# Expert sums, gates and selection by quarters instead of halves in a hybrid decoder with a product-key expert layer

## Chip, cores and metric

One core of one Trainium2 chip runs the whole program. The metric is device time in microseconds of one execution; the kernel before was timed three times, and its median is the number that the change is compared with. All profile rows come from one further execution, recorded by the hardware profiler.

## What is computed

Two layers; each adds a token mixer and an expert network to the residual stream `h` of 1040 tokens (16 meta tokens and 1024 real ones) by 1024 features. The mixer is left alone by the change. The expert network is this, cut from the reference:

```python
q = (xt @ wq).reshape(t, PEER_HEADS, 2, PEER_HALF)              # 8 heads, 2 halves of a key
s = jnp.einsum('thpd,hpnd->thpn', q, sub_keys)                  # 64 scores per half
s_top, i_top = lax.top_k(s, PEER_TOPK)                          # best 16 of each half
cand_s = s_top[:, :, 0, :, None] + s_top[:, :, 1, None, :]      # 256 sums
best_s, best_j = lax.top_k(cand_s..., PEER_TOPK)                # best 16 pairs = experts
g = jax.nn.softmax(best_s, axis=-1)
h_all = jnp.einsum('td,nd->tn', xt, u)                          # all 4096 experts
a = jax.nn.gelu(take_along_axis(h_all, idx)) * g
w = zeros((t, N_EXPERTS)).at[..., idx].add(a)
return w @ v
```

The kernel computes `gelu(xt @ u.T)` for all 4096 experts, multiplies it by a gate matrix that holds `g` at the chosen experts and 0 elsewhere, and multiplies the product by `v`.

## The kernel before

Tokens lie along the free dimension, in four quarters: 272 (with the meta tokens), 256, 256, 256 tokens; in the last layer the meta tokens are dropped and all four have 256. Two quarters form a half of the sequence, called `P` (the first two) and `Q` (the last two). All large products are made of three matmuls each, with operands split into a high and a low part of 32 bits (`wh`, `wl` for weights, `ah`, `al` for the gated hidden values). A weight block of 128x512 is loaded by `wpiece` (L296): the first time, ACT copies the high part (L273), POOL or DVE subtracts (L280, the engine is chosen by `split_on`) and the low part is also stored to DRAM (L292); at later times the block is loaded again, ACT copies the high part (L307) and the low part is loaded from DRAM (L310). All these transfers are issued from SP, in order.

For each half, in this order:

- `scores` (L960) computes the key scores of two heads for all token tiles.
- `route` (L987) works on DVE for two heads and all token tiles of the half: per tile and key half a top-16 search of five instructions (L997 to L1001), candidate sums (L1013 to L1020), a top-16 search over 64 candidates, softmax (the exponential is on ACT, L1032), and index arithmetic on 128x2048 arrays (L1067, L1070, L1074). It writes the expert's number in two parts, `mS` and `rS`, and the gate `gS`. There are four calls per half.
- `hidden` (L1094) makes `gelu(xt @ u.T)` in 32 row tiles of 128 experts, in one 512-wide matmul per step where both quarters have 256 tokens, else in a 272-wide and a 256-wide one. The result goes to the array `G` (L1113).
- `slots` (L1117) transposes `mS`, `rS`, `gS` by PE.
- `gates` (L1133) makes the gate matrix for 16 tokens: DVE compares with a ramp (L1142, 128x2048; L1144, 128x512) and multiplies by the high and the low part of the gates (L1146, L1147); PE multiplies the two one-hot matrices for each token. For `P` these are 32 matmuls of 32 columns (L1171); ACT copies the result, in part into a side tile, and POOL multiplies that into `G` (L1177). For `Q` (`wide`) they are 16 matmuls of 64 columns (L1159), and ACT and DVE (L1165) add two parts. Rows of `G` that `hidden` makes after the gate get multiplied by POOL (L1111). Calls of `gates` are spread over the rows of `hidden` from row 17 (`P`) or row 6 (`Q`) on.
- `values_steps` (L1185) sums over the experts: for four of the eight output tiles at a time it goes through the 32 rows of `G`, splits a row of both quarters (L1203 on ACT, L1204 on DVE), loads one `v` block of 128x512 and accumulates in PSUM (L1209). After the 32 rows the residual is updated (`hupdate`, L258).

The sum of `P` carries the normalisation (`apply`), the `scores` and the `route` calls of `Q` beside it, as pieces of a generator; `tc.issue_after` ties a piece to the subtraction of an earlier row (`LAG`), and `BUD` says how much of it may follow each row. The order of instructions within an engine's queue is otherwise chosen by a planner that follows a simulated timeline and takes ready work by its place in the program. Each queue then runs in that order. In the first layer the sum of `Q` is cut in two, with part of the next layer's projection between; in the last layer its second part is done for one quarter after the other, with the final normalisation behind.

```python
for r in range(32):                                               # values_steps
    wh, wl = wpiece(v_w[l][:, r, d0 * 128:d0 * 128 + 512], f"v{l}_{r}_{d0}" if reuse else None)
...
while cst and P.gated < P.sp.w and P.gated * (end - lo) < P.sp.w * (r + 1 - lo):   # hidden
    gates(P, G, *cst)
```

## Time and profile before

| | |
|---|---|
| median of 3 runs | 3380.03 us (3378.39 to 3394.43) |
| profiled execution | 3392.98 us, its span 3391.3 us |
| PE busy | 3157.8 us (93%) |
| DVE, ACT, POOL busy | 2172.3, 1381.1, 1091.0 us |
| mean granted clock of TensorE | 0.955 |
| moved by DMA | 651.27 MB, mean 192 GB/s |

The busy times are unions of recorded spans. A matmul's recorded span is longer than its distance to the next one, because matmuls overlap in the engine; the pace is read from rows that give the length of an unbroken series and its count. The span less the PE's busy time is 234 us; a granted clock below 1 in a stretch is a second kind of loss, which the busy time hides. The stretches of the expert network are, in us from the start: `hidden` of `P` 798 to 1061 and 2452 to 2724, sum of `P` 1061 to 1320 and 2724 to 2969, `hidden` of `Q` 1320 to 1535 and 2969 to 3182, sum of `Q` 1535 to 1800 (with a projection) and 3182 to the end.

### The profile page before, as it was taken

Reading aid. Unit: us, or ns where it says so; the run is one execution under the profiler, and the core shown is the slowest. Engines: PE = TensorE matmul, PEld = TensorE weight load, DVE = VectorE, ACT = ScalarE, POOL = GpSimd, SP = SyncE. Lnnn points to the kernel's source line nnn. Section 1 sums busy time; section 2 is a strip of 40 time slices with the busy share of each in tenths; the row PEclk is TensorE's granted clock in tenths of the full one; section 3 lists DMA queues with packets and bytes.
Section 4 is the critical chain, followed back from the end, with each engine's and each line's share of the span. In section 5 each row is a group of like instructions: output and inputs, shape, how many; then the busy total and the mean of one; then the engine's idle time right before and its main releaser. Section 6 shows DMA issues by size and latency. Waiting matters only on the chain.

```text
span 3391.3 us, 64331 instructions
## 1 busy us (share of the span) xinstructions
PE 3157.8 (93%) x22459; PEld 2647.5 (78%) x22459; DVE 2172.3 (64%) x7020; ACT 1381.1 (41%) x3278; POOL 1091.0 (32%) x1092
## 2 busy tenths in 40 slices
PE   7999999989788989999898999999898889999998
PEld 6686887679788988787775868876776678688788
DVE  4645446579896589663326454455698957976547
ACT  4534334433334434444344343344333344344355
POOL 4314022224475232131401231223245643313325
PEclk9899999989889999999997999999898899999999
DMA  8767774564324555445964687755753256554555
GB/s 284 236 202 247 257 245 146 174 217 164 125 88 158 182 178 189 163 152 191 331 232 151 210 274 241 232 170 167 251 173 125 94 179 221 183 189 151 180 173 156
DMA packets 397222, 651.27 MB, mean 192 GB/s; under 512 B 43536, under 2 KB 109152, under 8 KB 396896
## 3 DMA queue, kind: packets, MB, share of 16 engines
q1 hardware_dynamic: 396896, 647.16, 59.3%
q8 instruction: 176, 2.88, 0.4%
q14 instruction: 150, 1.23, 0.1%
HBM read 489.56 MB, written 157.42 MB: 191 GB/s over the span
## 4 chain that ended last, share of the span: by engine, by line
PE 59%; DVE 23%; DMA 6%; ACT 2%; issue 2%; POOL 1%; SPq 0%; POOLq 0%; DVEq 0%; ACTq 0%
PE b L1209 14%; PE b L1104 13%; PE b L334 12%; PE b L980 4%; DVE arena L1142 2%; DMA arena<-h 2%; PE b L704 2%; DVE arena_r L1204 2%; PE b L1159 2%; DVE arena L998 2%; DVE arena L999 2%; PE b L758 1%; DVE arena L1001 1%; PE b L619 1%; DVE arena L1147 1%
## 5 line engine op out<-in xcount | busy, mean ns | idle before, releaser
L280 POOL TENSOR_TENSOR arena_r<-arena,arena_r 128x512 fp32r<-128x512 f32 (+1 forms) x453 | 561.0, 1246 | 867.9 <-ACT arena_r L273 813.9
L1104 PE MATMUL b<-arena_r 128*128 128x512 f32 (+2 forms) x3840 | 782.3, 363 | 23.4 <-ACT arena L1113 13.5
L1209 PE MATMUL b<-arena_r 128*128 128x512 f32 (+2 forms) x4224 | 755.4, 337 | 36.5 <-DVE arena_r L1204 24.7
L1209 PEld LDWEIGHTS b<-arena_r 128*128 128x128 f32 x4224 | 643.8, 190 | 135.8 <-DVE arena_r L1204 41.9
L1104 PEld LDWEIGHTS b<-arena_r 128*128 128x128 f32 x3840 | 643.5, 197 | 123.4 <-ACT arena L1113 14.1
L334 PE MATMUL b<-arena_r 128*128 128x256 f32 (+1 forms) x4992 | 694.6, 293 | 33.8 <-ACT arena_r L273 10.2
L334 PEld LDWEIGHTS b<-arena_r 128*128 128x128 f32 x4992 | 635.1, 193 | 74.4 <-issue 21.8
L273 ACT ACTIVATE arena_r<-arena 128x512 fp32r<-128x512 f32 x456 | 285.1, 629 | 472.4 <-PE b L1104 124.4
L1204 DVE TENSOR_TENSOR arena_r<-arena,arena_r 128x512 fp32r<-128x512 f32 (+2 forms) x352 | 260.5, 751 | 230.9 <-ACT arena_r L1203 230.1
L307 ACT ACTIVATE arena_r<-arena 128x512 fp32r<-128x512 f32 x284 | 178.5, 631 | 327.4 <-PE b L1209 130.5
L980 PE MATMUL b<-arena_r 128*128 128x256 f32 (+1 forms) x1632 | 220.6, 291 | 15.3 <-DMA arena_r<-m_0l 5.3
L1142 DVE TENSOR_TENSOR arena<-arena 128x2048 f16<-128x2048 f16 x129 | 178.8, 1388 | 83.8 <-PE b L1159 83.7
L980 PEld LDWEIGHTS b<-arena_r 128*128 128x128 f32 (+1 forms) x1632 | 205.4, 190 | 27.9 <-DMA arena_r<-m_0l 7.3
L1177 POOL TENSOR_TENSOR arena<-arena 128x448 f32<-128x448 f32 (+20 forms) x129 | 144.2, 1123 | 150.8 <-DVE arena L1165 115.4
L1203 ACT ACTIVATE arena_r<-arena 128x512 fp32r<-128x512 f32 (+2 forms) x352 | 171.7, 502 | 25.2 <-PE b L1209 23.6
L256 POOL TENSOR_TENSOR arena<-arena 128x256 f32<-128x256 f32 (+2 forms) x105 | 90.7, 864 | 271.4 <-ACT arena L255 264.2
L280 DVE TENSOR_TENSOR arena_r<-arena,arena_r 128x256 fp32r<-128x256 f32 (+1 forms) x187 | 101.0, 546 | 92.1 <-ACT arena_r L273 71.2
L716 DVE TENSOR_TENSOR_SCAN arena<-arena,zf 128x384 f32<-128x384 f32 (+6 forms) x116 | 104.3, 903 | 79.0 <-ACT arena L711 77.8
L1111 POOL TENSOR_TENSOR arena<-arena 128x272 f32<-128x272 f32 (+25 forms) x86 | 95.1, 1110 | 158.4 <-DVE arena L1165 141.0
L422 ACT ACTIVATE arena<-b 128x256 f32<-128x256 f32 (+1 forms) x144 | 55.3, 384 | 202.0 <-PE b L334 201.2
L577 POOL TENSOR_TENSOR arena<-arena,mhalf 128x8 f32<-128x8 f32 (+3 forms) x43 | 63.6, 1479 | 210.5 <-DVE arena L574 143.3
L1171 PE MATMUL b<-arena 128*128 128x32 f16 x2080 | 83.5, 192 | 34.2 <-DVE arena L1142 15.9
(273 smaller groups left out, 4240.8 us busy)
## 6 DMA issues: line engine op xcount, KB each, us to landing
arena<-in_v_w_dram SPq DMA_DIRECT2D x288, 256.0 KB, 2.9
arena<-in_u_pk_dram SPq DMA_DIRECT2D x256, 256.0 KB, 3.0
arena_r<-a_0h SPq DMA_DIRECT2D x108, 256.0 KB, 3.7
arena_r<-a_0l SPq DMA_DIRECT2D x108, 256.0 KB, 4.0
arena_r<-a_1h SPq DMA_DIRECT2D x108, 256.0 KB, 3.3
arena_r<-a_1l SPq DMA_DIRECT2D x108, 256.0 KB, 3.9
arena<-m SPq DMA_DIRECT2D x92, 256.0 KB, 4.3
arena<-in_w_pk_dram SPq DMA_DIRECT2D x72, 256.0 KB, 4.3
```

The costliest lines, as they stand in the source:

```text
L273: ACT.activation(hi, src, AF.Copy)
L280: e.tensor_tensor(lo[:, a:b], src[:, a:b], hi[:, a:b].bitcast(F32), op=ALU.subtract)
L307: ACT.activation(hi, wload(src), AF.Copy)
L334: PE.matmul(ps, wt[:, ks], x.at(low, k, xo, sp.w), start=(k == 0 and i == 0), stop=(k == KT - 1 and i == 2))
L716: DVE.tensor_tensor_scan(keep[0:m, 0:wd][:, ::-1], keep[0:m, 0:wd][:, ::-1], zf[0:m, 0:1].to_broadcast([m, wd]), keep[0:m, wd:wd + 1], op0 ...
L980: PE.matmul(ps, yv(half, low, k, oo, m), wt[:, kk * 256:kk * 256 + 256], start=(k == 0 and i == 0 and e == 0), stop=(k == KT - 1 and i == ...
L1104: PE.matmul(ps, wt[:, ks], yv(h, low, k, 0, w // 2 if h is None else w), start=(k == 0 and i == 0), stop=(k == KT - 1 and i == 2))
L1142: DVE.tensor_tensor(Lh, iotaM.unsqueeze(1).to_broadcast([128, 4, 128, 4]), v4(P.mT, 128), op=ALU.is_equal)
L1177: POOL.tensor_tensor(G[:, 0:n, t0:t0 + 16], gt[:, 0:n], G[:, 0:n, t0:t0 + 16], op=ALU.mult)
L1203: ACT.activation(ah, G[:, r, o:o + w], AF.Copy)
L1204: last = DVE.tensor_tensor(al, G[:, r, o:o + w], ah.bitcast(F32), op=ALU.subtract)
L1209: PE.matmul(ps, wt[:, d * 128:d * 128 + 128], pr[low], start=(opens and r == 0 and i == 0), stop=(closes and r == 31 and i == 2))
```

## The change

Selection and gates are now made for one quarter at a time, and the sums too. In detail:

- `route` becomes `tops(P, half, cc)` (the first searches) and `combine(P, half, cc)` (the rest), each for four heads and the tiles of one quarter ("half" in the code is the first or second quarter of `P` or `Q`). The candidates and index arrays keep about their size: four heads by two or three tiles in place of two heads by four or five.
- Before `hidden` of `P` stands the selection of the first quarter alone. After 15 rows of `hidden` come `slots` of the first quarter and then `tops`, `combine`, `tops` of the second one; the gates of the first quarter are spread over rows 15 to 31.
- `values(l, P, G, half, ...)` sums one quarter. A 256-token quarter accumulates all eight output tiles in one pass over `G` (two tiles share a PSUM bank), so a row of `G` is split once and two `v` blocks are loaded per row; a 272-token quarter and the last quarter of all take two passes of four tiles.
- The sum of the first quarter carries `second`: the last `combine`, `slots` and all 16 calls of `gates` of the second quarter, plus `apply` for the third quarter. The sum of the second quarter carries `apply` for the fourth, the `scores` of `Q` and the selection of `Q`'s first quarter. `Q` goes the same way. In the last layer the final normalisation of three quarters runs beside the last sum.
- `gates`: one multiplication of 128x1024 for both parts of the gates; always 32 matmuls of 32 columns; rows of `G` that exist already are multiplied straight from PSUM by DVE; the rest is copied by ACT. The POOL product and the `wide` form go.
- PSUM rings, tile sizes and `BUD` (0.3 to 2.3), `PR` (17 to 15), `PEND` (29 to 31) change with it; `scores` copies two tiles of scores with one ACT instruction.

The core of the diff:

```diff
-    set_rings(d=(0, 1), o=(2,), a=(3, 4, 5, 6, 7), h=(0, 1, 6, 7), g=(2, 3), s=(2, 3, 4, 5), v=(4, 5, 6, 7, 2, 3))
+    set_rings(d=(0, 1), o=(2,), a=(3, 4, 5, 6, 7), h=(6, 7, 2, 3), g=(0, 1), s=(4, 5), v=(4, 5, 6, 7, 2, 3))
...
+    def gates(P, half, G, iotaM, iotaR):
...
+        R = sb([128, 4, 2, 32, 4], F16, "R")
+        DVE.tensor_tensor(R, R0.unsqueeze(2).to_broadcast([128, 4, 2, 32, 4]),
+                          P.gg[half][:, t0 // 4:t0 // 4 + 4].unsqueeze(3).to_broadcast([128, 4, 2, 32, 4]), op=ALU.mult)
...
         if n:
-            POOL.tensor_tensor(G[:, 0:n, t0:t0 + 16], gt[:, 0:n], G[:, 0:n, t0:t0 + 16], op=ALU.mult)
+            gv = G[:, 0:n, go:go + 16]
+            DVE.scalar_tensor_tensor(gv, pv[:, 0:n], 1.0 / GSC, gv, op0=ALU.mult, op1=ALU.mult)
...
+    def second(P, G, cst, tabs):
+        yield from combine(P, 1, 1, *tabs)
+        slots(P, 1)
+        yield 1.5
+        while P.gated[1] < P.parts[1][1].w:
+            gates(P, 1, G, *cst)
+            yield 3.0
+    def values(l, P, G, half, todo=iter(()), work=(), hs=None, group=8):
+        o, sp = P.parts[half]
+        w = sp.w
...
+        group = min(group, 4 if w > 256 else 8)
...
+        for d0 in range(0, 8, group):
...
+            for r in range(32):
...
+                done.append(DVE.tensor_tensor(al, G[:, r, o:o + w], ah.bitcast(F32), op=ALU.subtract).ins)
+                for d in range(group):
+                    if d % 4 == 0:
+                        wh, wl = wpiece(v_w[l][:, r, (d0 + d) * 128:(d0 + d) * 128 + 512], f"v{l}_{r}_{d0 + d}")
...
+                if len(done) > LAG:
+                    left = BUD * group / 8
+                    with tc.issue_after(done[-1 - LAG]):
+                        while left > 0:
+                            left -= next(todo, 99)
...
+            run(tops(P, 0, 0), combine(P, 0, 0, *tabs), tops(P, 0, 1))
+            scores(l, P, 3, (1,), "s")
+            run(combine(P, 0, 1, *tabs))
+        hidden(l, P, G, 0, PR, "h")
+        slots(P, 0)
+        run(tops(P, 1, 0), combine(P, 1, 0, *tabs), tops(P, 1, 1))
         hidden(l, P, G, PR, 32, "h", cst, PEND)
+        values(l, P, G, 0, second(P, G, cst, tabs), {20: lambda: apply(2 * l + 1, qs[2], gf, Y[0], rb)})
         Q = peer_setup(qs[2], qs[3])
...
+        values(l, P, G, 1, later(), work)
+        hidden(l, Q, G, 0, PR, "h")
+        slots(Q, 0)
+        run(tops(Q, 1, 0), combine(Q, 1, 0, *tabs), tops(Q, 1, 1))
+        hidden(l, Q, G, PR, 32, "h", cst, PEND)
...
+        values(l, Q, G, 0, second(Q, G, cst, tabs))
...
+        values(l, Q, G, 1, iter(()), {4 + 8 * i: lambda i=i: final(qs[i]) for i in range(3)}, hs, 4)
```

## Rows read from the trace of the kernel before

**Rows 1.** The page: span, and each engine's busy time, share and instructions

```profile
span 3391.3 us, 64331 instructions
...
PE 3157.8 (93%) x22459; PEld 2647.5 (78%) x22459; DVE 2172.3 (64%) x7020; ACT 1381.1 (41%) x3278; POOL 1091.0 (32%) x1092
```

**Rows 2.** Stretches: length, then PE, PEld, DVE, ACT, POOL busy, clock, DMA share, GB/s

```profile
798.00:1061.00 263.00, 224.61 (x2410) 219.85 (x2409) 232.00 (x648) 83.22 (x205) 151.32 (x109) 0.90 0.34 113
1061.00:1320.00 259.00, 243.62 (x1931) 237.78 (x1930) 195.31 (x931) 105.97 (x249) 89.11 (x68) 0.99 0.59 183
1320.00:1535.00 215.00, 212.65 (x1296) 172.90 (x1294) 146.65 (x439) 98.05 (x268) 62.32 (x72) 1.00 0.52 168
1535.00:1800.00 265.00, 253.36 (x1268) 210.02 (x1269) 84.78 (x140) 108.32 (x203) 44.29 (x60) 0.98 0.74 251
2452.00:2724.00 272.00, 232.62 (x1809) 187.31 (x1807) 245.01 (x748) 92.28 (x192) 153.41 (x112) 0.89 0.40 133
2724.00:2969.00 245.00, 235.08 (x1167) 192.50 (x1168) 188.99 (x882) 98.00 (x184) 90.20 (x64) 0.99 0.64 201
2969.00:3182.00 213.00, 210.82 (x1288) 172.35 (x1286) 146.02 (x418) 95.42 (x260) 60.94 (x60) 1.00 0.52 165
3182.00:3391.00 209.00, 194.50 (x1235) 174.54 (x1235) 124.51 (x214) 100.74 (x208) 65.76 (x70) 0.96 0.58 174
```

**Rows 3.** Timeline of PE: start, length and count of two unbroken series

```profile
1705.76 47.22 PE L1209 MATMUL b<-arena_r 128*128 128x512 f32 x204 [1.00 <-ACT arena_r L307]
...
3287.16 42.08 PE L1209 MATMUL b<-arena_r 128*128 128x256 f32 x356
```

**Rows 4.** Group on PE, 2592 to 2724 us: busy, mean ns, idle before, releasers

```profile
L1171 PE MATMUL b<-arena 128*128 128x32 f16 x1024 | 39.7, 192 | 17.5 <-DVE arena L1142 8.6 <-DVE arena L1147 6.2 <-DVE arena L1146 2.5
```

**Rows 5.** Shorter stretches, columns as in rows 2

```profile
1631.00:1706.00 75.00, 64.26 (x459) 59.00 (x458) 22.55 (x43) 29.11 (x59) 33.53 (x34) 0.98 1.00 357
2381.00:2452.00 71.00, 60.07 (x420) 56.90 (x420) 48.85 (x352) 24.25 (x50) 13.81 (x16) 0.89 0.81 261
2452.00:2570.00 118.00, 99.97 (x418) 78.80 (x416) 117.24 (x606) 43.09 (x68) 50.80 (x37) 0.93 0.51 170
2592.00:2724.00 132.00, 111.12 (x1301) 91.60 (x1299) 117.49 (x118) 44.19 (x114) 94.79 (x69) 0.86 0.31 102
```

**Rows 6.** Waits of ACT, 2452 to 2724 us: total us, times, longest

```profile
ACT arena L1032 <- DVE arena L1031: 33.2, 4, 13.9
```

**Rows 7.** Groups on DVE, 2592 to 2724 us, columns as in rows 4

```profile
L1142 DVE TENSOR_TENSOR arena<-arena 128x2048 f16<-128x2048 f16 x30 | 46.9, 1563 | 0.0
L1147 DVE TENSOR_TENSOR arena<-arena 128x512 f16<-128x512 f16 x30 | 28.9, 965 | 0.0
L1146 DVE TENSOR_TENSOR arena<-arena 128x512 f16<-128x512 f16 x30 | 27.4, 914 | 12.6 <-PE b L1171 12.5
L1144 DVE TENSOR_TENSOR arena<-arena 128x512 f16<-128x512 f16 x28 | 21.8, 804 | 0.1
```

**Rows 8.** Groups on DVE, 1370 to 1535 us, columns as in rows 4

```profile
L1142 DVE TENSOR_TENSOR arena<-arena 128x2048 f16<-128x2048 f16 x30 | 37.0, 1235 | 37.9 <-PE b L1159 37.8
L1146 DVE TENSOR_TENSOR arena<-arena 128x512 f16<-128x512 f16 x30 | 16.8, 558 | 0.0
...
L1165 DVE SCALAR_TENSOR_TENSOR arena<-b,arena 128x200 f32<-128x200 f32 x6 | 2.0, 354 | 0.5 <-ACT arena L1164 0.5
```

**Rows 9.** Groups on DVE, 1061 to 1320 us, columns as in rows 4

```profile
L1204 DVE TENSOR_TENSOR arena_r<-arena,arena_r 128x272 fp32r<-128x272 f32 x62 | 40.9, 661 | 29.3 <-ACT arena_r L1203 29.1
L1204 DVE TENSOR_TENSOR arena_r<-arena,arena_r 128x256 fp32r<-128x256 f32 x62 | 36.6, 590 | 3.4 <-ACT arena_r L1203 3.4
```

**Rows 10.** Group on POOL, 2724 to 2969 us, columns as in rows 4

```profile
L280 POOL TENSOR_TENSOR arena_r<-arena,arena_r 128x512 fp32r<-128x512 f32 x59 | 83.6, 1421 | 132.3 <-ACT arena_r L273 109.2 <-DMA arena<-in_v_w_dram 18.1 <-DMA arena_r<-m_3l 3.2
```

**Rows 11.** DMA issues over the whole span: count, KB each, median us to landing

```profile
arena<-in_v_w_dram SPq DMA_DIRECT2D x288, 256.0 KB, 2.9
```

**Rows 12.** Group on ACT over the whole span, columns as in rows 4

```profile
L307 ACT ACTIVATE arena_r<-arena 128x512 fp32r<-128x512 f32 x284 | 178.5, 631 | 327.4 <-PE b L1209 130.5 <-PE b L1104 90.7 <-issue 62.0
```

More of the change, by code (lines that the diff above doesn't have):

```diff
@@ L959, in scores @@
     def scores(l, P, c, halves, ring):
[L961 to L968 removed]
+        pairs = []
+        for half in halves:
+            tiles = list(enumerate(P.parts[half][1].tiles))
+            if len(tiles) == 3:
+                POOL.memset(sv(P, half, c)[:, 0], 0.0)
+                pairs.append((half, tiles[0:1]))
+            pairs.append((half, tiles[-2:]))
         bks = [ps1(ring) for _ in pairs]
@@ new lines, in scores, with top16 @@
+        for bk, (half, tiles) in zip(bks, pairs):
+            j, m, n = tiles[0][0], tiles[0][1][1], len(tiles)
+            ACT.activation(sv(P, half, c)[0:m, j:j + n], bk[0:m, 0:n * 256].rearrange("p (j a n) -> p j a n", a=4, n=64),
+                           AF.Copy)
+    def top16(s, val, idx):
+        DVE.max(val[:, 0:8], s)
+        DVE.max_index(idx[:, 0:8], val[:, 0:8], s)
+        DVE.match_replace(s, val[:, 0:8], s, -3.0e38)
+        DVE.max(val[:, 8:16], s)
+        DVE.max_index(idx[:, 8:16], val[:, 8:16], s)
@@ new lines, in tops, with combine @@
+    def tops(P, half, cc):
+        nt = len(P.parts[half][1].tiles)
+        V = sb([128, 3, 8, 16], F32, "V")
+        I = sb([128, 3, 8, 16], U32, "I")
+        P.V[half, cc] = V, I
+        for a in range(8):
+            for j in range(nt):
+                top16(sv(P, half, 2 * cc + a // 4)[:, j, a % 4, :], V[:, j, a], I[:, j, a])
+                yield 1.3
+    def combine(P, half, cc, startT, pidxT):
+        nt = len(P.parts[half][1].tiles)
+        ng = 4 * nt
+        V, I = P.V.pop((half, cc))
@@ L1114, in hidden, with slots @@
             P.rows = r + 1
-            while cst and P.gated < P.sp.w and P.gated * (end - lo) < P.sp.w * (r + 1 - lo):
-                gates(P, G, *cst)
-    def slots(P):
-        sp = P.sp
-        for j, (o, m) in enumerate(sp.tiles):
+            w0 = P.parts[0][1].w
+            while cst and P.gated[0] < w0 and P.gated[0] * (end - lo) < w0 * (r + 1 - lo):
+                gates(P, 0, G, *cst)
+    def slots(P, half):
+        for j, (o, m) in enumerate(P.parts[half][1].tiles):
             tp = ps1("g").bitcast(F16)[:, 0:256].rearrange("p (a b) -> p a b", a=2)
@@ new lines, in gates @@
+        R0 = sb([128, 4, 32, 4], F16, "R0")
+        DVE.tensor_tensor(R0, iotaR.unsqueeze(1).to_broadcast([128, 4, 32, 4]), v4(P.rT[half], 32), op=ALU.is_equal)
+        R = sb([128, 4, 2, 32, 4], F16, "R")
+        DVE.tensor_tensor(R, R0.unsqueeze(2).to_broadcast([128, 4, 2, 32, 4]),
+                          P.gg[half][:, t0 // 4:t0 // 4 + 4].unsqueeze(3).to_broadcast([128, 4, 2, 32, 4]), op=ALU.mult)
+        n = P.rows
+        ps = ps1("g")
+        for i in range(16):
+            b, t = i // 4, i % 4
+            for part in range(2):
+                PE.matmul(ps[:, i * 32:(i + 1) * 32], Lh[:, b, :, t], R[:, b, part, :, t], start=(part == 0),
+                          stop=(part == 1))
@@ L1215, in values_steps @@
+            for d in range(group):
+                ps = accs[d][0]
                 if hs is not None:
-                    DVE.tensor_tensor(hs[:, d0 + d, o:o + w], hs[:, d0 + d, o:o + w], ps, op=ALU.add)
+                    DVE.tensor_tensor(hs[:, d0 + d], hs[:, d0 + d], ps, op=ALU.add)
                     continue
@@ L1288, in tile_trunk @@
             if q == 3:
-                for c in range(P.ns - 1):
+                for c in range(3):
                     scores(l, P, c, (0,), "d")
@@ L1341, in tile_trunk, with later @@
-        for _ in todo:
-            pass
-        split_on(POOL)
-        hidden(l, Q, G, 0, HQ, "h")
-        slots(Q)
-        split_on(*QSPL)
-        set_rings(g=(2, 3, 4, 5))
-        hidden(l, Q, G, HQ, 32, "h", cst, QE)
-        set_rings(g=(2, 3))
+        work = {0: lambda: apply(2 * l + 1, qs[3], gf, Y[1], rb2)}
+        scored = []
+        def later():
+            for cc in range(2):
+                for gen in (tops(Q, 0, cc), combine(Q, 0, cc, *tabs)):
+                    while len(scored) < 2 * cc + 2:
+                        yield 99
+                    yield from gen
```

299 lines of the change are left out of this document (102 added, 197 removed).

## Prediction

> **What bounds the kernel now.** I read the page's totals first, then the stretches of the expert network, then the groups and waits inside those where PE is not full. PE is busy 3157.8 us of 3391.3, besides its weight loads (78%) nothing is over 64% [rows 1], so what can be won is PE's idle and slowed time, and this lies in few stretches [rows 2]. The pace of an undisturbed series is 47.22 us / 204 = 0.2315 us for a 512-wide matmul and 42.08 / 356 = 0.118 us for a 256-wide one [rows 3]: two narrow ones (0.236) cost 2% more than a wide one, and PE doesn't mind the halving. With these, `hidden` of P in the second layer needs 768 x 0.2315 = 178 us plus 32 gates at 39.7/32 = 1.24 us [rows 4] = 40, so 218, but takes 272; in the first layer 1536 x 0.122 (between 0.118 and 0.118 x 272/256) = 187 + 41 = 228 against 263. Here DVE is busy 245 of 272 and 232 of 263 us, and the granted clock is 0.89 and 0.90 [rows 2]. First DVE selects (117 busy of 118, [rows 5]) while ACT, in order, stands before the softmax for 33.2 us in four waits [rows 6] and weight copies queue behind it. Then DVE makes gates: 117.5 of 132 us, PE waits 17.5 us for it [rows 4, 5] at clock 0.86. Loss: 54 + 35 = 89 us. `hidden` of Q loses next to nothing: 213 and 215 us, PE busy 211 and 213, clock 1.00 [rows 2].
>
> **The change, part by part.** The sum is made against the profiled execution (3392.98 us), 13 us above the median 3380.03; I subtract the same difference from both.
>
> *Hidden of P.* Half of the gates and the last `combine` leave it. DVE's four selection calls of the second layer fill 48.85 + 117.24 = 166 us [rows 5], less some 9 for other work: 39 each. A new call of four heads on half the tiles has as many searches, so 39 too: of it 14 for `tops`, 25 for `combine` (estimate: 16 of its 24 searches move with `tops`, and searches are a little over half). After 2452 us DVE then has 39 + 14 + 25 + 14 = 92 and 16 gates. PE needs 178 + 16 x 1.24 = 198. DVE is no longer longer; what stays is about two of the four softmax waits (16 us) and a late start of the gates, because `combine` can write `mS`, `rS`, `gS` only when `slots` has read them at row 15. I take 14 us: 212 (**-60**) and in the first layer 187 + 21 + 14 = 222 (**-41**). Bounds: 198 (no wait) and 228 (all 33 us of waits kept, little else).
>
> *Sum of P's first quarter.* PE: 768 x 0.118 = 91 + 20 for gates = 111 (272-wide: 97 + 21 = 118). Beside it DVE does the moved work. A gate there has four instructions: the two comparisons, one multiplication of 128x1024, which the trace doesn't have, and a product of up to 512 elements from PSUM, which it has only up to smaller sizes. Beside POOL they are 1.563 and 0.804; the multiplication lies between 0.965 (doubling is free) and 0.914 + 0.965 = 1.88 [rows 7], and I take 1.54, nearer to the two it replaces, less one start; the PSUM product lies between 0.354 and 0.354 x 512/200 = 0.91 [rows 8], I take 0.65. That is 4.56 us, 73 for 16. With `combine` 25, `slots` 2, 32 subtractions of 0.59 [rows 9] = 19 and `apply` (16 instructions, as 0.59) 9, it is 128; in the first layer, where 272 tokens need two passes, 64 x 0.661 = 42 instead of 19: 151. So DVE, not PE, sets 129 and 151. Rows of a quiet POOL give 1.235 for the large comparison and 0.558 for a multiplication instead of 1.563 and 0.914 [rows 7, 8]; by them DVE needs about 97 and 110 and PE sets 111 and 118. I take the stretched ones, as POOL is then at 64 x 1.42 = 91 us [rows 10] of 129, 70%, as in the gate stretch (94.8 of 132). Each `v` block also stores its low part from SP behind POOL's subtraction; later loads queue behind it, which the same 129 us cover (64 blocks of 512 KB both ways, 33.5 MB, 260 GB/s).
>
> *Sum of P's second quarter.* 91 + 384 score matmuls x 0.118 = 136. DVE has `tops` and `combine` twice (78) and 28, with POOL nearly idle: hidden behind PE. The DMA load is 33.5 MB of `v` (256 KB raw and 256 KB low part for each of 64 blocks), 8.4 of score weights, 3 of residuals: 45 MB, 321 GB/s. I add 4: 140. Both quarters of P: 269 against 245 (**+24**), 291 against 259 (**+32**).
>
> *Hidden of Q.* Half of the gates leave: 178 + 20, and 5 for the selection that now runs here (DVE: a rest of 40, then 53, then 16 gates of under 3 us; 147 us busy now, PE full): 203 (**-12, -10**).
>
> *Sums of Q.* Raw `v` loads rise from 288 [rows 11] to 512, low loads from 96 to 384, all on SP's one queue. A quarter needs 32 x 1.049 MB; PE would take 91 us, 369 GB/s. The highest the trace shows is 357 GB/s at a DMA share of 1.00 [rows 5], so 94 us. First layer: 91 + 20 = 111, the projection's 75 as now [rows 5], 94, 1: 281 against 265 (**+16**). Second: 111; the last sum with 6.3 MB of final normalisation beside it is 39.8 MB / 357 GB/s = 112; 13 behind the last matmul, untouched: 236 against 209 (**+27**).
>
> *At nothing:* ACT copies 224 more blocks at 0.631 [rows 12]; a row then has 2 x 0.63 + 0.4 = 1.7 us of ACT under 2.8 of PE. If PE's queue of five ready blocks runs dry, each costs up to 0.63. The rings, smaller tiles and merged score copies lie behind full PE; the missing POOL product is off PE's path.
>
> Sum: -60 - 41 + 24 + 32 - 12 - 10 + 16 + 27 = **-24 us**: 3369 profiled, **3356** against the median, -0.7%. A difference under 0.5% (17 us) can't be told from none; the three runs alone differ by 16.
>
> The Trainium skill, "DMA: Bandwidth & Descriptors", section "Where 436 GB/s comes from", puts a core's limit to HBM at about 358 GB/s, and the section's measurements before it reach 425 with the other core idle. By 425 the sum would be 21 us lower; the trace shows 357 and no more.
>
> **Rivals.** *A, POOL doesn't stretch DVE:* PE sets the first quarters, 111 and 118; -18 - 33 = -51, so 3305. For it: the product that POOL made goes, and the quiet rows. Against it: the new home of the gates is where POOL splits every `v` block. *B, hidden of P isn't freed:* the planner's order, or gates waiting for `combine`, which itself waits for `slots` at row 15, keep 30 us of loss per stretch instead of 14; +32, so 3388, no change. This is also the case where the change doesn't do what it says. *C, slower, by turns in the first quarter:* DVE's two-input work (gates 16 x (1.235 + 0.558 + about 0.92) = 43, subtractions 19, half of `combine`, `apply`: 84) and POOL's 91 follow one another: 175 and, with 23 more, 198, so +93: 3449. It decides against the change once the two first quarters together exceed 280 + 24 = 304. Against it: in the gate stretch DVE and POOL together are recorded busy for 212 of 132 us [rows 5]; for it: that record may hold waiting, as the quiet rows suggest. The Trainium skill, "SBUF — State Buffer", section "Who interferes with whom", says that a VectorE operation with two inputs in SBUF and a GpSimd one that reads SBUF exclude each other for a whole instruction. By that rule C's time holds; the stretched rows agree in kind, and no row shows strict turns. *D, slower, DMA:* the sums get 310 GB/s, between 261 at a share of 0.81 and 357 [rows 5]: 108 for a quarter (+14), 128 for the last (+16), 145 and 115 for the others (+18): 3404. For it: SP's one queue and head-of-line waits.
>
> **Numbers.** The forecast has 0.32, A 0.14, B 0.25, C 0.14, D 0.15. Faster 0.46, no change 0.25, slower 0.29. The range takes in A, B and D and leaves out most of C: 3300 to 3415; the forecast's own, from its bounds, is 3330 to 3375.
>
> **What would show it.** `hidden` of P at 205 to 230 us with clock above 0.93; the first quarter's sum at 125 to 155 us with DVE over 90% busy and PE waiting for L-lines of the gates or the subtraction; the second at about 140; Q's last sum with DMA share near 1. The forecast is wrong if the first quarters run at PE's 111 (A) or over 165 (C), if `hidden` of P stays above 235 (B), or if PE waits for `v` or its low part in Q's sums for more than 20 us (D).

## The result, and the profile after

The changed kernel took **3426.05 us** (median of 4 runs, 3419.03 to 3430.83) against 3381.87 for the kernel before (median of 4 runs): ratio **1.0122** [1.009, 1.0155], slower by 1.2%, which is clear of the noise. The forecast was 3356 and a range up to 3415. The profiled execution spans 3429.1 us against 3391.3, 37.8 more.

The page's totals, which answer to [rows 1], and the two DMA issues that answer to [rows 11]:

```profile
span 3429.1 us, 70511 instructions
...
PE 3172.4 (93%) x25373; PEld 2755.2 (80%) x25373; DVE 2000.8 (58%) x6689; ACT 1378.0 (40%) x3122; POOL 866.1 (25%) x901
...
arena<-in_v_w_dram SPq DMA_DIRECT2D x512, 256.0 KB, 4.3
...
arena_r<-v_0l SPq DMA_DIRECT2D x192, 256.0 KB, 4.5
```

VectorE and POOL are busy for less time than before, and still the span is longer: no total explains it. The stretches do. Columns as in [rows 2]: length, PE, PEld, DVE, ACT and POOL busy, clock, DMA share, GB/s. First layer: `hidden` of P up to the gates, with gates, P's first and second quarter, `hidden` of Q, Q's first quarter, projection, Q's second quarter.

```profile
790.00:887.00 97.00, 91.35 (x730) 90.99 (x728) 84.42 (x451) 34.71 (x68) 45.44 (x32) 0.96 0.53 177
887.00:1007.00 120.00, 120.00 (x1367) 119.04 (x1366) 63.24 (x107) 38.56 (x107) 64.64 (x49) 1.00 0.46 152
1007.00:1164.00 157.00, 129.41 (x1293) 125.05 (x1292) 145.06 (x233) 65.86 (x143) 100.21 (x64) 0.92 0.68 221
1164.00:1313.00 149.00, 140.22 (x1152) 136.92 (x1150) 92.85 (x653) 69.78 (x134) 3.15 (x4) 0.99 0.92 313
1313.00:1520.00 207.00, 201.91 (x1284) 163.42 (x1285) 90.07 (x320) 69.64 (x144) 12.81 (x22) 0.97 0.53 170
1520.00:1635.00 115.00, 113.53 (x1304) 111.24 (x1304) 83.50 (x213) 56.58 (x114) 8.13 (x20) 1.00 0.89 297
1635.00:1719.00 84.00, 66.88 (x472) 62.50 (x471) 20.84 (x46) 29.69 (x60) 39.12 (x42) 0.92 0.98 337
1719.00:1817.00 98.00, 95.59 (x786) 92.76 (x784) 17.38 (x40) 51.60 (x104) 2.99 (x14) 1.00 1.01 361
```

Second layer: `hidden` of P, P's two quarters, `hidden` of Q, Q's two quarters.

```profile
2485.00:2684.00 199.00, 198.32 (x1288) 160.12 (x1287) 128.46 (x408) 66.36 (x138) 107.37 (x80) 1.00 0.54 177
2684.00:2825.00 141.00, 120.73 (x1283) 118.06 (x1282) 129.48 (x206) 52.11 (x105) 96.23 (x61) 0.93 0.72 234
2825.00:2983.00 158.00, 142.52 (x1159) 137.84 (x1157) 93.77 (x657) 70.88 (x139) 5.21 (x7) 1.00 0.90 304
2983.00:3193.00 210.00, 203.21 (x1286) 163.41 (x1287) 89.96 (x322) 69.31 (x144) 12.22 (x22) 0.97 0.54 173
3193.00:3304.00 111.00, 110.71 (x1290) 109.36 (x1289) 75.11 (x187) 52.43 (x103) 0.95 (x2) 1.00 0.89 295
3304.00:3414.00 110.00, 99.80 (x809) 95.93 (x808) 38.52 (x98) 62.34 (x134) 7.61 (x10) 1.00 1.01 353
```

Against [rows 2], in us (the lengths after go from the first to the last matmul of each part, so they are within a microsecond or two of the windows above; "behind" is a gap after the second quarter):

| stretch | layer 1 | forecast | layer 2 | forecast |
|---|---|---|---|---|
| hidden of P | -47 | -41 | -73 | -60 |
| P's sums | +47.5 (156.6 and 145.0, 5 behind) | +32 (151, 140) | +55 (141.7 and 155.3, 3 behind) | +24 (129, 140) |
| hidden of Q | -7 | -12 | -4 | -10 |
| Q's sums, projection | +32 | +16 | +27 | +27 |
| attention and scores, ahead of hidden of P | -7 | 0 | +14.6 | 0 |

They add to +38. Three losses have to be explained: P's first quarter, where DVE and POOL are both busy and PE is not; P's second quarter with what follows it; and Q's sums.

### The profile page after: what moved, and what is told of

Its sections match the earlier page's. It is cut to its first block, busy times and chain, and to the rows that moved or that the text cites. A ratio compares the mean times of both kernels' runs of the same rounds, so it can differ in the third digit from the quotient of the medians.

```text
span 3429.1 us, 70511 instructions
## 1 busy us (share of the span) xinstructions
PE 3172.4 (93%) x25373; PEld 2755.2 (80%) x25373; DVE 2000.8 (58%) x6689; ACT 1378.0 (40%) x3122; POOL 866.1 (25%) x901
## 4 chain that ended last, share of the span: by engine, by line
PE 41%; DVE 13%; DMA 9%; issue 4%; ACT 1%; SPq 1%; POOL 1%; POOLq 0%; DVEq 0%; ACTq 0%
PE b L1107 15%; PE b L1205 9%; PE b L332 6%; PE b L1159 3%; PE b L981 2%; DMA arena<-in_v_w_dram 2%; DMA arena<-h 1%; DVE arena_r L1198 1%; PE b L702 1%; DMA arena<-in_w_pk_dram 1%; DVE arena L1147 1%; DMA arena_r<-v_4l 1%; DVE arena L991 1%; DVE arena L992 1%; DVE arena L994 1%
## 5 line engine op out<-in xcount | busy, mean ns | idle before, releaser
L1205 PE MATMUL b<-arena_r 128*128 128x256 f32 (+1 forms) x6144 | 791.1, 288 | 46.7 <-DVE arena_r L1198 16.2
L1205 PEld LDWEIGHTS b<-arena_r 128*128 128x128 f32 x6144 | 759.0, 193 | 61.9 <-DVE arena_r L1198 18.9
L1107 PE MATMUL b<-arena_r 128*128 128x512 f32 (+2 forms) x3840 | 754.3, 356 | 19.6 <-DVE arena L993 9.3
L332 PE MATMUL b<-arena_r 128*128 128x256 f32 (+1 forms) x4992 | 701.1, 294 | 39.2 <-ACT arena_r L271 14.2
L1107 PEld LDWEIGHTS b<-arena_r 128*128 128x128 f32 x3840 | 626.2, 191 | 121.4 <-ACT arena L1116 5.9
L332 PEld LDWEIGHTS b<-arena_r 128*128 128x128 f32 x4992 | 640.5, 195 | 78.9 <-issue 23.1
L305 ACT ACTIVATE arena_r<-arena 128x512 fp32r<-128x512 f32 x576 | 360.8, 630 | 515.8 <-PE b L1107 131.2
L271 ACT ACTIVATE arena_r<-arena 128x512 fp32r<-128x512 f32 x392 | 245.1, 629 | 381.8 <-PE b L1107 115.6
L1198 DVE TENSOR_TENSOR arena_r<-arena,arena_r 128x256 fp32r<-128x256 f32 (+1 forms) x320 | 176.0, 555 | 255.0 <-ACT arena_r L1197 254.7
L254 POOL TENSOR_TENSOR arena<-arena 128x256 f32<-128x256 f32 (+1 forms) x126 | 97.1, 770 | 678.7 <-ACT arena L253 674.5
L981 PE MATMUL b<-arena_r 128*128 128x256 f32 (+1 forms) x1632 | 229.5, 296 | 31.5 <-DVE arena_r L376 7.1
L1159 PEld LDWEIGHTS <-arena 128*128 128x128 f16 x4128 | 148.5, 118 | 38.2 <-issue 30.4
L1159 PE MATMUL b<-arena 128*128 128x32 f16 x4128 | 159.4, 191 | 20.9 <-DVE arena L1152 20.7
L1197 ACT ACTIVATE arena_r<-arena 128x256 fp32r<-128x256 f32 (+1 forms) x320 | 129.2, 408 | 77.4 <-PE b L1205 77.1
L1164 DVE SCALAR_TENSOR_TENSOR arena<-b,arena 128x512 f32<-128x512 f32 (+16 forms) x129 | 78.8, 611 | 85.7 <-PE b L1159 81.4
```

What stands on the lines that cost most here:

```text
L271: ACT.activation(hi, src, AF.Copy)
L305: ACT.activation(hi, wload(src), AF.Copy)
L332: PE.matmul(ps, wt[:, ks], x.at(low, k, xo, sp.w), start=(k == 0 and i == 0), stop=(k == KT - 1 and i == 2))
L981: PE.matmul(ps, yv(half, low, k, o, m), wt[:, kk * 256:kk * 256 + 256], start=(k == 0 and i == 0 and e == 0), stop=(k == KT - 1 and i == 2 ...
L1107: PE.matmul(ps, wt[:, ks], yv(h, low, k, 0, w // 2 if h is None else w), start=(k == 0 and i == 0), stop=(k == KT - 1 and i == 2))
L1159: PE.matmul(ps[:, i * 32:(i + 1) * 32], Lh[:, b, :, t], R[:, b, part, :, t], start=(part == 0), stop=(part == 1))
```

## The experiments

Line numbers shift by a few between kernels. "First sums" are P's first quarter in layer 1 and 2. Kernels that ran several times differ by up to 21 us from run to run, so the total of a single run is read no closer than that, and the stretches carry the argument.

**1. No POOL in the first sums.** The low part of `v` is not subtracted and stored there, but a stored block of `u` is read in its place.

```diff
+        if key is not None and key[0] == "v":
+            a, b, c = key[1:].split("_")
+            ACT.activation(hi, wload(src), AF.Copy)
+            SP.dma_start(lo.bitcast(F32), kept[f"u{a}_{b}_{int(c) // 4}"][1])
+            return hi, lo
```

> Of every v block the low part is replaced by a stored low part of u of the same size, so neither POOL's subtraction nor the store of the low part is left in the first quarter's sum of P (the output is thereby another); DVE's instructions stay. Theory (DVE's two-input work and POOL's subtraction stretch each other): the first quarters' sums fall from 157 and 142 us to 118 to 128 and 111 to 120, the gates' 128x1024 product from 0.95 and 1.22 us to under 0.72, the whole to about 3360. Rival 1 (DVE simply has too much to do there): the sums stay above 140 and 130. The second quarters' sums (145, 155) stay as they are under both, as their transfers do.

Measured: 3343.31 us (one run), 83 less than the changed kernel. The first sums are 118.3 and 112.3 us, TensorE's own 118 and 111. VectorE's groups in the first one, in the changed kernel and then in this one (count | busy us, mean ns | idle before):

```profile
L1198 DVE TENSOR_TENSOR arena_r<-arena,arena_r 128x272 fp32r<-128x272 f32 x60 | 45.6, 773 | 7.5 <-ACT arena_r L1197 7.4
L1147 DVE TENSOR_TENSOR arena<-arena 128x2048 f16<-128x2048 f16 x16 | 25.6, 1605 | 0.0
L1152 DVE TENSOR_TENSOR arena<-arena 128x1024 f16<-128x1024 f16 x16 | 15.1, 949 | 0.0
L1150 DVE TENSOR_TENSOR arena<-arena 128x512 f16<-128x512 f16 x16 | 13.6, 855 | 0.0
L1164 DVE SCALAR_TENSOR_TENSOR arena<-b,arena 128x512 f32<-128x512 f32 x16 | 10.9, 678 | 1.9 <-PE b L1159 1.9
```

```profile
L1203 DVE TENSOR_TENSOR arena_r<-arena,arena_r 128x272 fp32r<-128x272 f32 x60 | 26.5, 446 | 14.8 <-ACT arena_r L1202 14.7
L1152 DVE TENSOR_TENSOR arena<-arena 128x2048 f16<-128x2048 f16 x16 | 19.3, 1214 | 0.0
L1169 DVE SCALAR_TENSOR_TENSOR arena<-b,arena 128x512 f32<-128x512 f32 x16 | 10.9, 682 | 0.8 <-PE b L1164 0.8
L1157 DVE TENSOR_TENSOR arena<-arena 128x1024 f16<-128x1024 f16 x16 | 10.8, 681 | 0.0
L1155 DVE TENSOR_TENSOR arena<-arena 128x512 f16<-128x512 f16 x16 | 7.1, 451 | 0.0
```

Each operation with two inputs in SBUF falls (773 to 446, 1605 to 1214, 949 to 681, 855 to 451 ns). The product that reads one input from PSUM stays: 678 and 682. PE's waits in that sum, in the changed kernel, were 16.2 us for the subtraction and 10.0 for the gates' product:

```profile
PE b L1205 <- DVE arena_r L1198: 16.2, 13, 4.3
PE b L1159 <- DVE arena L1152: 10.0, 6, 3.7
```

Here they are under 2 us together. The two first sums as a whole, with the columns of [rows 2]; the lines for the changed kernel stand above:

```profile
1006.00:1124.00 118.00, 116.13 (x1287) 114.56 (x1286) 94.42 (x235) 66.47 (x145) 3.30 (x4) 1.00 0.88 298
2630.00:2742.00 112.00, 111.07 (x1287) 109.37 (x1286) 80.35 (x209) 54.72 (x109) 0.73 (x1) 1.00 0.91 301
```

In the changed kernel PE stood for 27.6 of 157 us, at a granted clock of 0.92; here for 2 of 118, at 1.00. Nearly the same VectorE instructions take 94 us of records in place of 145. The edit also takes the 128 stores out of the first sums; that is separated in 3.

**2. No low parts read.** On each later use the high part of `v` stands for the low one: 384 transfers fewer.

```diff
         kh, kl = kept[key]
+        if key[0] == "v":
+            ACT.activation(hi, wload(src), AF.Copy)
+            return hi, hi
```

> On its second to fourth use a v block's high part stands in for its low part, which is not loaded (the output is thereby another): 384 transfers of 256 KB fewer, the same matmuls. Theory (these sums are bound by DMA): the second quarters' sums of P fall from 145 and 155 us to 137 to 143, the last sums of Q from 97 and 110 to 91 to 96, the projection between from 85 to 80; the whole falls by 45 to 60 us to about 3375. Rival 2 (they are bound by ACT's copies, by DVE or by the emptying of PSUM at their ends): each stays within 4 us, the whole within 10.

Measured: 3364.28 us (one run). P's second quarters fall from 145.0 and 155.3 to 139.0 and 147.1, Q's last ones from 97.1 and 110.3 to 93.9 and 97.7. That is 30 us in the sums. The attention is 14 us shorter in this run, which the edit doesn't touch, and no part of the total beyond the sums is claimed. In the seven other kernels that leave P's second quarters as they are (3, 4, 5, 7, 8, 9, 10) these took 144.3 to 147.2 and 153.0 to 159.1 us, so the 6 and 8 lie outside that spread, but not by much. So the low parts' transfers cost these sums 3 to 13 us each; 147 is still 11 above TensorE's 136, which stays open.

**3. Stores left out, subtractions kept.** POOL works in the first sums as in the changed kernel, but its results are not stored.

```diff
-            if key is not None:
+            if key is not None and key[0] == "v":
+                a, b, c = key[1:].split("_")
+                kept[key] = (None, kept[f"u{a}_{b}_{int(c) // 4}"][1])
+            elif key is not None:
```

> The changed kernel, in which POOL's subtractions in the first sum of each layer stay, but their results are not stored: the later sums read a stored low part of u in the place of v's (the transfers stay as many, the low part of v in the later sums is left out). Theory (VectorE and POOL stretch each other): the first sums stay within 8 us of 156.6 and 141.7, POOL's subtraction above 1500 ns, the gates' product above 900 ns. Rival (SP stands at each store until POOL is done, 70 us in each first sum, and the loads queued behind it come late): the first sums fall to 120 to 130 and 112 to 125 us although POOL's subtraction keeps its 1600 ns. If both, something like 140 and 128.

Measured: 3418.86 us (one run). First sums 153.2 and 141.3, within 4 us of the changed kernel. The rival falls: SP's 70.3 us before the stores in the changed kernel, first line, cost little or nothing. POOL's group in this kernel's first sum, and the sum as a whole:

```profile
SPq L290 <- POOL arena_r L278: 70.3, 48, 7.0
```

```profile
L278 POOL TENSOR_TENSOR arena_r<-arena,arena_r 128x512 fp32r<-128x512 f32 x60 | 92.9, 1565 | 47.8 <-ACT arena_r L271 47.2 <-PE b L1208 0.5
```

```profile
1003.00:1156.00 153.00, 128.75 (x1288) 125.04 (x1287) 147.70 (x239) 66.94 (x145) 96.15 (x64) 0.91 0.44 127
```

**4. No gates in the first sums.** P's second quarter is not gated.

```diff
+        if not gated:
+            return
         while P.gated[1] < P.parts[1][1].w:
```

> The 16 gate calls of P's second quarter are left out (that quarter stays ungated, the output is thereby another); POOL's subtraction and the store of the low part stay. Theory (DVE and POOL stretch each other): the first quarters' sums fall to 104 to 116 and 94 to 104 us, POOL's subtraction from 1.62 us to under 1.45. Rival 3 (POOL's subtraction, or the stores that wait for it in SP's queue, set the pace by themselves): they stay above 130 and 120, the subtraction at 1.6.

Measured: 3371.0 us (one run). First sums 120.7 and 119.7, above the 94 to 116 of the theory and below the rival's bound in layer 1, at it in layer 2; POOL's subtraction is 1446 and 1414 ns, just under the theory's 1.45 us. So the gates are worth 36 and 22 us there, but something else holds the sums above TensorE's own 97 and 91. The trace of the second one has ACT, whose copy of the high part POOL's subtraction needs, standing for `v`'s raw blocks:

```profile
ACT arena_r L271 <- DMA arena<-in_v_w_dram: 33.5, 38, 2.3
```

**5. The combine earlier.** `slots` of the first quarter at row 12 in place of 15, and the last `combine` of P in `hidden`, not beside the first sum.

```diff
-        hidden(l, P, G, 0, PR, "h")
+        hidden(l, P, G, 0, 12, "h")
         slots(P, 0)
-        run(tops(P, 1, 0), combine(P, 1, 0, *tabs), tops(P, 1, 1))
-        hidden(l, P, G, PR, 32, "h", cst, PEND)
+        run(tops(P, 1, 0), combine(P, 1, 0, *tabs), tops(P, 1, 1), combine(P, 1, 1, *tabs))
+        hidden(l, P, G, 12, PR, "h")
+        hidden(l, P, G, PR, 32, "h", cst, PEND)
```

> slots of P's first quarter goes to row 12 of hidden, and the last combine of P (25 to 35 us of DVE) from the first quarter's sum to before row 12's successors, where DVE is 55% busy and PE full. Theory (DVE's load sets the first sum): the sums fall by 18 to 30 us each, to 127 to 139 and 112 to 124, hidden of P stays within 6 us, the whole falls by 30 to 55 us to about 3385. Rival 3 (POOL sets it): the sums fall by under 10 us each. Rival 4 (gates come too late in hidden): hidden of P grows by more than 12 us and the whole falls by under 15.

Measured: 3416.3 us, ratio to before 1.0093 [1.0064, 1.0123]. First sums 144.9 and 130.6 (-12, -11), between the theory's 18 to 30 and rival 3's under 10; `hidden` of P 11 and 6 longer: most of it is moved, not saved.

**6. The low parts made ahead, in attention.** Nothing is left out; 64 blocks per layer are loaded, split and stored behind the output products.

```diff
             hupdate(2 * l + 1, j, sp, ht, ps)
+            ahead(l, n)
...
+        for r, d in list(itertools.islice(early, n)):
+            wpiece(v_w[l][:, r, d:d + 512], f"v{l}_{r}_{d // 128}")
```

> The changed kernel, in which the low part of v is made and stored during the attention of each layer (64 blocks of 256 KB loaded, rounded by ScalarE, subtracted by POOL and stored, spread over the output products of the second to fourth quarter); the first sum then reads it back as the later ones do, and POOL has nothing to do there. Nothing is left out. Theory: the first sums fall to 118 and 112 us as without POOL's subtractions (-68 us), attention pays 5 to 15 us in each layer for 33.5 MB more and 64 more operations of ScalarE and POOL: 3426 - 68 + 20 = 3378, between 3360 and 3390. Rival (attention has no room: TensorE is busy for 95% there and weights come through the same buffers): attention grows by 30 us or more in each layer, the total stays above 3415.

Measured: 3491.35 us, ratio 1.0312 [1.0281, 1.0343]. The first sums do fall, to 115.9 and 112.5, with all their gates and products: the cause is confirmed a second time, with nothing left out. But in layer 1 `hidden` of P begins 65 us later (855.2 against 790.6), and layer 2's attention, with its scores, takes 751 against 668, so the rival about attention is right. PE's busy time and the granted clock show it, 200 to 632 us, changed kernel and then this one:

```profile
200.00:632.00 432.00, 414.66 (x3115) 327.41 (x3115) 221.27 (x517) 174.84 (x456) 99.00 (x124) 0.97 0.68 217
```

```profile
200.00:632.00 432.00, 395.46 (x2856) 314.06 (x2855) 221.88 (x487) 185.74 (x472) 151.26 (x157) 0.92 0.72 236
```

**7. Q's quarters summed together again.** 512 rows wide, two passes of four output tiles, all gates of Q in its `hidden`.

```diff
-        hidden(l, Q, G, PR, 32, "h", cst, PEND)
+        hidden(l, Q, G, 8, 20, "h", cst, 20)
+        slots(Q, 1)
+        hidden(l, Q, G, 20, 32, "h", cst, PEND, 1)
...
-        values(l, Q, G, 0, second(Q, G, cst, tabs))
+            both(l, Q, G, 0)
```

> The changed kernel with one part undone: Q's two quarters are again summed together, 512 rows wide, in two passes of four output tiles, so v is read once for Q and not twice, and all of Q's gates and its last combine lie in its hidden values, where VectorE was busy for 48 of the last 114 us. Theory (the pace of 256-wide products and the second reading of v cost Q's sums 32 and 31.5 us): the stretch of sums and projection falls from 295.6 to about 264 us in layer 1, Q's sums from 236 to about 205 us in layer 2, hidden values of Q grow by 7 to 10 us in each layer (the gating they had before), together about -45 us against the changed kernel, 3380 us. Rival 1 (the selection of Q by quarters is what was dear): the sums stay above 285 and 230 us, the total at 3420. Rival 2 (32 gates and a combine don't fit beside hidden values): hidden Q grows by over 25 us in each layer and the total stays above 3410.

Measured: 3399.61 us (one run), -26 in place of -45. Q's sums with projection fall to 262 and, second layer, to 196 us before the end's 13. `hidden` of Q grows to 223.5 and 227.0, by 16 and 18, since 16 gates take TensorE itself some 20 us wherever they stand, which my expectation had left out.

Experiments 6 and 7 in one kernel were expected at 3333 us if the two gains add, and near 3380 if attention takes the first one back. Measured: 3441.48 us (5 runs, 3434.55 to 3453.48), ratio to before 1.0183 [1.0155, 1.0211]. The first sums are 115.8 and 111.3, Q's sums with projection 263 and in layer 2 192, about as in 6 and 7; but against 7 `hidden` of P begins 66 us later in layer 1, and layer 2's attention with scores takes 720 in place of 665. Attention takes back more than the gain.

**8. The same, and `hidden` of Q begins in free PSUM banks.** In the changed kernel TensorE stands before `hidden` of Q:

```profile
PE b L1107 <- DVE arena L993: 9.3, 2, 4.9
```

The sum of P's second quarter leaves its eight output tiles in four banks, 6, 7, 2, 3 in layer 1, and `hidden` takes the banks in that order. The instructions that empty them (L258) stand in VectorE's queue among the searches of the selection; the profile names a search (L993) as the last releaser, but the emptying runs through the same time (durations, then first and last start), where the kernel before waits 0.3 us:

```profile
L258 DVE TENSOR_TENSOR arena<-arena,b x8: 389/402/414, 1312.7 to 1331.7; 128x256 f32<-128x256 f32 x8
```

```profile
PE b L1104 <- DVE arena L260: 0.3, 1, 0.3
```

In layer 2 the changed kernel waits as long in the same place, but the trace names other releasers, a weight's high part and a transpose of `slots` that stands for `combine`:

```profile
PE b L1131 <- DVE arena L1039: 5.0, 1, 5.0
PE b L1107 <- ACT arena_r L305: 3.1, 1, 3.1
...
PE b L1107 <- DMA arena_r<-u_0l: 0.7, 1, 0.7
...
PE b L1107 <- DVE arena L258: 0.2, 1, 0.2
```

The edit (`P.last` holds the banks of P's last sum; ahead of `hidden` of P the old order is set again):

```diff
+        busy = P.last[-4:]
+        set_rings(h=tuple([b for b in range(2, 8) if b not in busy] + busy[0:2]))
         hidden(l, Q, G, 0, 8, "h")
```

> The kernel with Q's sums together (3399.6 us) and one thing more: the hidden values of Q begin in PSUM banks that the last sum of P did not use. Theory (after a sum of eight output tiles TensorE stands until VectorE, whose queue holds the selection, has emptied the four banks: 9.1 us of waits at the start of hidden Q in layer 1 and a gap of 5 and 3 us before it): hidden Q falls from 223.5 and 227.0 to about 217 us, the gap to under 1 us, -8 us in each layer, 3384 us. Rival (hidden Q waits for the applied rows or for weights, and the banks are only what the trace names last): no change, 3395 to 3400 us.

Measured: **3353.86 us**, ratio to before **0.9902** [0.9888, 0.9917]: faster than both kernels, by 1% against the one before. From the end of P's second quarter to the end of `hidden` of Q it is some 13 and 15 us shorter. The rest of the 46 between this kernel and the single run of 7 lies in parts that are the same in both (10 in layer 2's attention, 5 in the scores behind it).

**9. The banks alone, on the changed kernel.**

```diff
+        busy = P.last[-4:]
+        set_rings(h=tuple([b for b in range(2, 8) if b not in busy] + busy[0:2]))
         hidden(l, Q, G, 0, PR, "h")
```

> The changed kernel, and in it only that the hidden values of Q begin in PSUM banks that the last sum of P did not use; everything else is as changed, Q's sums by quarters too. Theory (the emptying of eight output tiles behind VectorE's selection costs 9 us of waiting and, by the clock of 0.83 to 0.91 behind it, some 4 us more in each layer): the gap before hidden Q and hidden Q together fall by 13 us in each layer, as they did with Q's sums together (4.9 + 223.5 to 0.4 + 215.6), and the total by 26 us, to 3400 us, ratio to the kernel before 1.005. Rival (the 46 us that the same edit gave there came mostly from stretches that it doesn't touch, and these differ from run to run): the gap falls, but the total stays above 3415.

Measured: 3398.95 us (12 runs, 3385.52 to 3402.54), ratio to before 1.0035 [1.002, 1.005]; the theory had said 3400. From P's last matmul to the end of `hidden` of Q: 1308.5 to 1520.4 = 211.9 in the changed kernel, 1300.6 to 1497.9 = 197.3 here; 212.4 and 196.8 in layer 2. TensorE's clock is the second part of it. In the changed kernel, around the wait:

```profile
1300.00:1320.00 20.00, 15.15 (x94) 13.72 (x93) 20.00 (x172) 6.60 (x12) 1.46 (x2) 0.83 0.76 261
1320.00:1360.00 40.00, 35.54 (x142) 28.33 (x142) 35.10 (x172) 16.77 (x27) 3.79 (x5) 0.91 0.60 189
```

and with free banks, where PE never stood still:

```profile
1300.00:1340.00 40.00, 40.00 (x178) 32.52 (x178) 39.93 (x250) 19.64 (x37) 5.73 (x7) 1.00 0.72 233
```

So 9 us of waiting cost 15; the other 6 go with the lower of the two clock levels (1.2 in place of 2.4 GHz), granted for part of the 50 us from the wait on. In layer 2 the 9 us of waits shown in 8 are gone too (0.4 left) and the clock around them is 1.00 in place of 0.89. That the banks are their cause rests there on the experiment alone; the planner orders the queues anew for another order of banks, and by what step the waits went is open.

**10. Low parts ahead, elsewhere.** On kernel 8, layer 2's low parts are made in layer 1's `hidden` and sums of Q, one block at a time, where POOL is idle.

```diff
             P.rows = r + 1
+            if nxt:
+                ahead(l + 1, 1)
```

> The kernel before in this list, and the low part of layer 2's v made and stored during layer 1's hidden values and sums of Q, one block per row of experts or per two, where POOL was idle and DMA moved 150 to 214 GB/s. Nothing is left out. Theory (VectorE and POOL stretch each other in the first sum, and POOL's work costs nothing where VectorE has slack and TensorE doesn't wait): the first sum of layer 2 falls from 140 to about 113 us, layer 1's Q keeps its time within 6 us, together -24 us, 3360 us. Rival (the cost of making the parts ahead is what it was in attention, 63 us for 64 blocks, wherever it is put): layer 1's Q grows by 40 us or more and the total stays above 3395.

Measured: 3404.68 us, ratio 1.0062 [1.0047, 1.0078]; the rival is right. Layer 2's first sum goes from 142.7 to 111.7, but layer 1's `hidden` of Q goes from 215.6 to 243.5 and the sums with projection from 261.8 to 300.9, together +67 for 64 blocks. `hidden` of Q in kernel 8 and in this one:

```profile
1302.00:1518.00 216.00, 215.84 (x1808) 177.43 (x1806) 159.42 (x516) 78.69 (x174) 32.34 (x36) 1.00 0.54 170
```

```profile
1303.00:1547.00 244.00, 225.19 (x1810) 181.42 (x1809) 165.53 (x515) 91.41 (x202) 71.35 (x67) 0.97 0.68 214
```

Besides PE and its weight loads no engine is busy for more than 68%, and the DMA is at 214 GB/s; PE waits, 8.6 us of it for `u`'s low part. In the second half of the stretch SP stands 34.8 us for raw blocks of `u`, 12.8 for POOL's subtraction and 12.7 until a stored block has landed and its buffer is free; in kernel 8 it stood there almost only for PE to use up what was loaded (70.9 us).

**11. Both layers' low parts ahead, in layer 1's attention one at a time.**

```diff
-        braid(stick(), window(), linear())
+        braid(stick(), window(), linear(), made(0 if l else (10, 18, 18, 18)[A.b0 // 2]))
```

> As the one before, and layer 1's low parts made during layer 1's attention, but one at a time among its steps (10, 18, 18 and 18 in the four quarters) and not in bunches of two or three behind each output product. Theory (attention paid 63 us because the blocks came in bunches, when TensorE's own weights stood behind them in the same buffers): attention grows by 10 us or less, the first sum of layer 1 falls to 118 us, together -28 us, 3332 us, ratio to the kernel before 0.985. Rival (attention has no room for 64 blocks): it grows by 30 us or more, total above 3360.

Measured: 3418.61 us, ratio 1.0086 [1.0071, 1.01]. Attention with the scores ends at 854.4 us against 785.6, again about 1 us for each block. It was not the bunches. In all the places tried, 64 blocks through the shared weight buffers and SP's one queue cost 55 to 83 us. Buffers or a queue of their own were not tried, so which of the two it is stays open.

## Why the prediction was wrong

**Hidden of P was right**, and a little better than said: 216.7 and 199.3 us (forecast 222 and 212), clock 0.96 to 1.00, PE without a gap once the gates begin. (In the kernel before, 196 of the first layer's 1536 matmuls run ahead of 798 us, between the scores; my 228 us of need for that stretch overlooked them, the 222 for the changed kernel isn't touched by it.) Rival B is out: VectorE did stand 12.3 and 19.6 us for the transposes of `slots`, and PE didn't wait for it.

**The step that failed is P's two sums, +56 forecast, +102.5 measured**: 18 from the first quarters, 20 from the second, 8 from the gaps behind them. Of the 62 us between the forecast's -24 and the measured +38 these are 46; Q's sums in the first layer are 16, `hidden` of Q 11, attention and scores 7, and `hidden` of P gave 19 back. No one part made the change a loss: the first quarters' 18 alone would have left it at -6.

*First quarter.* I took VectorE's stretched durations, added them up, and left POOL's 91 us as something that fits beside (129 and 151; measured 141.7 and 156.6). The runs show rival C's mechanism: VectorE's two-input operations and POOL's subtraction keep each other waiting, and taking POOL's work away brings the sums to TensorE's own time (experiments 1 and 6). How far they take strict turns can be tried by adding the undisturbed durations of both. VectorE's operations with two inputs in SBUF, as in experiment 1, are 27 + 19 + 11 + 7 as shown there and 18 in smaller groups (the applied rows, the last `combine`), 82 us in layer 1 and about 66 in layer 2, where the subtractions are half as many. POOL's subtraction is 1297 ns, close to its shortest, where VectorE has less of such work:

```profile
L924 POOL TENSOR_TENSOR arena_r<-arena,arena_r x64: 1263/1297/2005, 1301.6 to 1833.9; 128x512 fp32r<-128x512 f32 x64
```

(shortest, middle and longest, experiment 10), so the 60 in the sum are 78. 82 + 78 = 160 and 66 + 78 = 144, against 156.6 and 141.7. The same sum without the gates' 37 gives 123 in layer 1 for experiment 4 (120.7 measured), but 107 in layer 2, where 119.7 was measured. There ACT's wait for `v`'s blocks says that loads held the sum, so the agreement in its first layer may be luck, and strict turns are not shown. What the records do show is waiting inside them: VectorE's 145 us are 94 in experiment 1, and POOL's 60 subtractions are 97 where 78 would do. Rival C's own sign, over 165 us for a quarter or over 304 for both, did not come (156.6, together 298). It had priced the sums at 175 and 198, because it took stretched values again, 1.42 for POOL and 0.59 and 0.66 for VectorE's subtractions (0.42 and 0.45 undisturbed), and 0.92 for a multiplication that takes 0.68.

The Trainium skill, "SBUF — State Buffer", section "Who interferes with whom", says that a VectorE instruction with two inputs in SBUF contends with a GpSimd instruction that reads SBUF, and that one with at most one SBUF input, outside VectorE's two-port modes, doesn't. The trace agrees in both halves: 773 against 446 ns for the subtraction, 678 against 682 for the product from PSUM. By that rule, taken as strict turns and with the undisturbed durations, the two sums come out within 4 us; but these durations are from experiments 1 and 10, and I did not have them all. I had given it a chance of 0.14, with stretched ones.

*Second quarter, and the gap.* 145 and 155 in place of 140: by experiment 2 the low parts' transfers alone are worth 6 and 8 us; the other 7 in layer 2 stay open. What I had no term for is the change's eight output tiles per sum. They are emptied by an engine whose queue is full of selection, and the next stage starts in just those banks: 15 us in layer 1 (experiment 9), part of it in the gap, part in `hidden` of Q, where -7 was measured for -12. In layer 2 the same edit gave 15 us too, by a step that is open; `hidden` of Q had -4 there for -10. With free banks it is -17 and -16, gap included.

**Q's sums:** second layer 110.9, 110.3 and 15 against 111, 112 and 13, right. First layer 113.7, 85 for the projection, 97.1 against 111, 75 and 94. The projection's 10 us are the miss: I had it "as now", at 357 GB/s and a share of 1.00 [rows 5], that is, already bound by transfers; now it moves 337 GB/s at clock 0.92. With Q's sums together again (7, 8) it takes 77 us, and 80 to 85 in all the kernels that sum Q by quarters and make no low parts beside it, so the quarter sums around it made it longer; by what was not tried. Rival D was too dark: the quarter behind the projection runs at 361 GB/s with a share of 1.01. The ceiling I took from [rows 5] holds over sums of this length, though "357 and no more" does not for shorter stretches: 20 us have up to 372 GB/s before and 385 after. The Trainium skill, "DMA: Bandwidth & Descriptors", section "Where 436 GB/s comes from", gives 358 GB/s as a core's limit to HBM; the trace agrees over the two sums (361 and 353), and the 425 of the same page's measurements was not reached.

**No term at all** had the attention behind a sum of eight tiles: with the scores +14.6 in layer 2, where PE waits 9.5 us once for the emptying, and 0.4 before. Changed kernel, then before:

```profile
PE b L617 <- DVE arena L258: 9.5, 1, 9.5
```

```profile
PE b L503 <- DVE arena L260: 0.4, 1, 0.4
```

The wait stays in experiment 9 (9.3 us), as only Q's banks were changed there. How much of the 14.6 it explains is open: this stretch took 661 to 675 us in the runs that leave it as in the changed kernel.

So much of two of the three losses is taken back in kernel 8, which undoes a part of the change, as Q's sums and gates are again those of a half, keeps the selection by quarters and P's halved gates, and beats both. The third, the 68 us that experiment 1 takes off the first sums, is still in it.

## What to carry to other kernels

Where two engines keep each other waiting, as VectorE's two-input operations and POOL's subtraction did here, don't let one fit beside the other: their undisturbed durations added came within 4 us of both first sums. An operation that takes longer in one stretch than in another (773 against 446 ns) holds waiting in its record, and the busy time with it. When a stage is made to end with more output tiles in PSUM, ask which banks the next stage opens first and what stands in the queue of the engine that empties them: another order of the banks was worth 27 of the 44 us lost here. Work that "fits where an engine is idle" has to pass through the same buffers and the same DMA queue as TensorE's weights, and in every place tried here it cost more than it saved.

## What was not expected of the hardware

A wait of 9 us cost 15: the granted clock was 0.83 and 0.91 in the 60 us around and behind it, and 1.00 without it. And 64 blocks made ahead cost 65 and 83 us in attention (66 and 55 with Q's sums together), 67 in Q and 69 in attention one by one, though in the two stretches shown DMA was at 214 and 236 GB/s of the 361 reached elsewhere and POOL idle for most of the time.
